# Adding two arrays and a GELU: a narrow load moved to the end of the loads

## The chip, the cores and the metric

The kernel runs on one core of a Trainium2 chip. The metric is the device time of one execution in microseconds (us), as a median of several runs. The profile is of one execution; its span is the time from the first to the last recorded event on the core.

## The reference

Two float32 arrays of 1024 x 4096 are added, and the tanh form of GELU is taken of the sum:

```python
def reference(x, y):
    z = x + y
    return (0.5 * z * (1 + np.tanh(np.sqrt(2 / np.pi) * (z + 0.044715 * z ** 3)))).astype(np.float32)
```

Every element is used once. 33.55 MB are read and 16.78 MB written.

## The kernel before

The arrays are taken as flat memory. On the chip the work is a plane of 128 partitions by TOT = 32,768 float32 columns, and `rows` (L90) says where a range of columns lies in memory: three blocks, columns 704 to 16,384 first, then 16,384 to 32,768, then columns 0 to 704 last. A row of a transfer is contiguous in memory.

There are two large tiles. `zt` (L128) has all 32,768 columns: x is loaded into it, the sum overwrites it, the GELU overwrites that, and the stores read it. `yt` (L129) has half the columns, 16,384: y's first half is loaded into it, and when its adds are done, y's second half is loaded over it. `ps` (L130) is a PSUM tile of 4,096 columns into which ScalarE copies some chunks of x, so that VectorE's add reads one operand from there and not both from the same memory as GpSimd's adds.

Transfers. x, y and the output are each moved in three pieces of 704, 15,680 and 16,384 columns. All nine are issued by SyncE (SP) on one queue, in the order of the list `sp` (L178): y's narrow piece, y's 15,680, x's narrow piece, x's 15,680, x's second half, y's second half; then the stores: the 15,680 columns, the narrow piece, the second half. SP works this list off in order, and an issue that waits holds up those behind it. y's second half waits for the adds of the chunks that still read `yt` (the `needs` entry of `load_y`, L186). A store waits for the GELUs of its columns (L193). After the build, `begin_early` (L9) puts the first two issues ahead of the start-up barrier, and `wait_late` (L23) lets only ScalarE wait for the last store.

Arithmetic. The columns are cut into 20 chunks (`chunks`, L103): two of 1,024, seven of 2,048, then from column 16,384 on 512, 1,536, six of 2,048, 1,024 and two of 512. Each chunk is added by VectorE (`on_vector`, L105) or GpSimd (`on_gpsimd`, L106: chunks 7, 8 and 12); chunk 7's add is held until chunk 1's is done (`held`, L108). Chunks 2 to 6 and 9 to 11 are first copied to PSUM by ScalarE (`copies`, L104). ScalarE also takes all GELUs. Its order, `on_scalar` (L107), is written out by hand: the five copies of the first half, the GELUs of chunks 0 and 1, the three copies of the second half, then the GELUs of chunks 2 to 19. Each engine takes its list in order; a loop (L200 to L210) only emits the instructions in an order that respects `needs`, and semaphores make the engines wait at run time.

Of the kernel before, what the change touches and what calls it, by code (L numbers as in the profile page):

```python
# [8 lines left out]
def begin_early(nc, count):  # L9


    head, body = (b.instructions for b in nc.main_func.blocks[:2])
    SP = mybir.EngineType.SP
    moved = [i for i in body if i.engine == SP and isinstance(i, mybir.InstDMACopy)][:count]
    assert not any(i.sync_info and i.sync_info.on_wait for i in moved)
    assert all(i.regs_accessed() == ((), ()) for i in moved)
    at = next(k for k, i in enumerate(head) if i.engine == SP)
    for k, i in enumerate(moved):
        body.remove(i)
        head.insert(at + k, i)  # L20
# [45 lines left out]
@with_exitstack  # L66
def kernel(
    ctx: ExitStack,
    tc: tile.TileContext,
    x: bass.AP,  # L70
    y: bass.AP,
    out: bass.AP,
):

    nc = tc.nc  # L80
    P = nc.NUM_PARTITIONS
    fp32 = mybir.dt.float32
    act = mybir.ActivationFunctionType

    N, D = x.shape
    assert N % P == 0
    TOT = N // P * D
    blocks = [(704, 16384), (16384, TOT), (0, 704)]

    def rows(array, lo, hi):  # L90
        flat, at = array.rearrange("n d -> (n d)"), 0
        for f, e in blocks:
            if f <= lo and hi <= e:
                own = flat[P * at : P * (at + e - f)].rearrange("(p c) -> p c", p=P)
                return own[:, lo - f : hi - f]
            at += e - f
        raise AssertionError((lo, hi))

    HALF = TOT // 2
    xloads = [704, 15680, HALF]  # L100
    yloads = [704, 15680, HALF]
    stores = [704, 15680, HALF]
    chunks = [1024, 1024] + [2048] * 7 + [512, 1536] + [2048] * 6 + [1024, 512, 512]  # L103
    copies = {2: 0, 3: 2048, 4: 0, 5: 2048, 6: 0, 9: 0, 10: 512, 11: 2048}  # L104
    on_vector = [0, 1, 2, 3, 4, 5, 6, 9, 10, 11, 13, 14, 15, 16, 17, 18, 19]  # L105
    on_gpsimd = [7, 8, 12]  # L106
    on_scalar = [("copy", c) for c in (2, 3, 4, 5, 6)] + [("gelu", 0), ("gelu", 1)] + [("copy", c) for c in (9, 10, 11)] + [("gelu", c) for c in range(2, 20)]  # L107
    held = {7: 1}  # L108

    def ranges(sizes):  # L110
        ends = [sum(sizes[: i + 1]) for i in range(len(sizes))]
        assert ends[-1] == TOT
        return [(e - f, e) for e, f in zip(ends, sizes)]

    xr, yr, sr, cr = (ranges(r) for r in (xloads, yloads, stores, chunks))
    C = len(cr)
    assert sorted(on_vector + on_gpsimd) == list(range(C))
    assert sorted(c for what, c in on_scalar if what == "gelu") == list(range(C))

    def over(rs, lo, hi):  # L120
        return [i for i, (a, b) in enumerate(rs) if a < hi and b > lo]

    pool_sb = ctx.enter_context(tc.tile_pool(name="xz", bufs=1))
    pool_y = ctx.enter_context(tc.tile_pool(name="y", bufs=1))
    pool_ps = ctx.enter_context(tc.tile_pool(name="ps", bufs=1, space=bass.MemoryType.PSUM))

    one = pool_sb.tile([P, 992], fp32, tag="one", name="one")
    zt = pool_sb.tile([P, TOT], fp32, tag="z", name="z")  # L128
    yt = pool_y.tile([P, HALF], fp32, tag="y", name="y")  # L129
    ps = pool_ps.tile([P, 4096], fp32, tag="ps", name="ps")  # L130
    adds = {}

    def in_psum(c):
        a, b = cr[c]
        return ps[:, copies[c] : copies[c] + b - a]

    def load_x(i):
        a, b = xr[i]
        nc.sync.dma_start(out=zt[:, a:b], in_=rows(x, a, b))  # L139

    def load_y(i):
        a, b = yr[i]
        o = a % HALF
        nc.sync.dma_start(out=yt[:, o : o + b - a], in_=rows(y, a, b))  # L144

    def store(i):
        a, b = sr[i]
        nc.sync.dma_start(out=rows(out, a, b), in_=zt[:, a:b])

    def copy(c):  # L150
        a, b = cr[c]
        nc.scalar.copy(out=in_psum(c), in_=zt[:, a:b])  # L152

    def add(c):
        a, b = cr[c]
        o = a % HALF
        eng = nc.gpsimd if c in on_gpsimd else nc.vector
        first = in_psum(c) if c in copies else zt[:, a:b]
        ins = eng.tensor_add(out=zt[:, a:b], in0=first, in1=yt[:, o : o + b - a])  # L159
        adds[c] = ins.ins  # L160
        if c in held:
            tc.add_manual_dep(
                ins.ins,
                adds[held[c]].name,
                mybir.DependencyInfo(mybir.DependencyClass.Sync, mybir.DependencyReason.DATA),
                reason="GpSimd's adds run beside VectorE adds that read one operand from PSUM",
            )

    def gelu(c):
        a, b = cr[c]  # L170
        nc.scalar.activation(out=zt[:, a:b], in_=zt[:, a:b], func=act.Gelu_apprx_tanh)  # L171

    def earlier_user(c):
        lo, hi = copies[c], copies[c] + chunks[c]
        before = [k for k in copies if k < c and copies[k] < hi and copies[k] + chunks[k] > lo]
        return [(add, k) for k in before]

    sp = [(load_y, 0), (load_y, 1), (load_x, 0), (load_x, 1), (load_x, 2), (load_y, 2)]  # L178
    sp += [(store, i) for i in (1, 0, 2)]
    pool = [(add, c) for c in on_gpsimd]  # L180
    dve = [(add, c) for c in on_vector]
    acts = [(gelu if what == "gelu" else copy, c) for what, c in on_scalar]

    needs = {
        load_x: lambda i: [],
        load_y: lambda i: [(add, c) for c in over(cr, yr[i][0] - HALF, yr[i][1] - HALF)],  # L186
        copy: lambda c: [(load_x, i) for i in over(xr, *cr[c])] + earlier_user(c),
        add: lambda c: [(load_x, i) for i in over(xr, *cr[c])]
        + [(load_y, i) for i in over(yr, *cr[c])]
        + [(copy, k) for k in copies if k == c]  # L190
        + [(add, k) for h, k in held.items() if h == c],
        gelu: lambda c: [(add, c)],
        store: lambda i: [(gelu, c) for c in over(cr, *sr[i])],  # L193
    }
    queues = [sp, pool, acts, dve]
    done = set()
    with tc.manual_schedule():
        nc.vector.memset(one[:, :1], 0.0)  # L198
        nc.scalar.activation(out=one[:, :1], in_=one[:, :1], func=act.Gelu_apprx_tanh)  # L199
        while any(queues):  # L200
            moved = False
            for q in queues:
                while q and all(n in done for n in needs[q[0][0]](q[0][1])):
                    fn, arg = q.pop(0)
                    fn(arg)
                    done.add((fn, arg))
                    moved = True
                    if q is not sp:
                        break
            assert moved, [q[:1] for q in queues]  # L210

    ctx.close()
    tc.close()
    tc.compile()  # L214
    begin_early(nc, 2)
    wait_late(nc)
# [30 lines left out]
```

## Time and profile before

| | us |
|---|---|
| median of 3 runs | 120.46 (120.14 to 120.53) |
| the profiled execution | 120.13 |
| its span | 118.6 |
| VectorE busy (DVE) | 29.1 |
| ScalarE busy (ACT) | 44.1 |
| GpSimd busy (POOL) | 13.8 |
| 2,048-column GELU, mean | 1.895 |
| 2,048-column add on VectorE, mean | 2.28 |
| 2,048-column add on GpSimd, mean | 4.54 |

Times of instructions are from the span's start. A group's line in the profile gives line, engine, operation, the tile written and the tiles read with their shapes, and how often. In a timeline the first two numbers are start and length in us, and the bracket is the idle time before it with what ended it. "SPq" is SyncE's queue, whose work is to issue transfers. For a transfer, "to landing" is the time from its issue until its semaphore says that all of it has arrived; on a queue with other transfers ahead of it, that includes their time. The packet records are the trace's list of the single packets, each with its start, length and size; a packet here is one row of a transfer.

### The profile page before, as it was taken

To read this page: it belongs to the slowest core of one execution; us is meant where nothing else is said; L and a number is where in the kernel's file an instruction comes from. 1 tells how busy PE (TensorE), PEld (TensorE's weight loads), DVE (VectorE), ACT (ScalarE), POOL (GpSimd) and SP (SyncE) were. 2 spreads that over 40 slices of the span, in tenths; PEclk is the share of its full clock that TensorE was granted. 3 is DMA by queue.
4 is the path that set the end of the run, shared out by engine and by line. 5 is a ranking of instruction groups with operands and counts; after the bars stand their busy time and mean duration, and the time that the engine had idled before them with its cause. 6 is when DMAs were issued, how large, how long until landed. Compare 5 with 4: busy or idle time off the path is not lost.

```text
span 118.6 us, 119 instructions
## 1 busy us (share of the span) xinstructions
DVE 29.1 (25%) x18; ACT 44.1 (37%) x30; POOL 13.8 (12%) x7
## 2 busy tenths in 40 slices
DVE  0000000000000099994000000009999920000000
ACT  5000000000000196792059999904799980000000
POOL 0000000000000029970000000009500000000000
DMA  9779977999789888988899889977997789988891
GB/s 460 338 338 571 444 338 338 460 571 444 338 360 656 354 354 376 663 376 354 354 597 464 354 354 508 552 338 338 529 486 338 338 385 517 619 354 354 354 663 44
DMA packets 1296, 50.33 MB, mean 424 GB/s; under 512 B 144, under 2 KB 144, under 8 KB 528
## 3 DMA queue, kind: packets, MB, share of 16 engines
q1 hardware_dynamic: 1296, 50.33, 98.6%
HBM read 33.55 MB, written 16.78 MB: 424 GB/s over the span
## 4 chain that ended last, share of the span: by engine, by line
DMA 55%; DVE 14%; ACT 10%; DVEq 1%; ACTq 0%; SPq 0%; issue 0%
DMA z<-in_x_dram 33%; DMA y<-in_y_dram 21%; DVE z L159 14%; ACT z L171 10%; DVEq L214 1%; ACTq L214 0%; SPq L139 0%; DVEq L159 0%; SPq L144 0%
## 5 line engine op out<-in xcount | busy, mean ns | idle before, releaser
L171 ACT ACTIVATE z<-z 128x2048 f32<-128x2048 f32 (+3 forms) x20 | 29.7, 1555 | 5.6 <-DVE z L159 5.6
L152 ACT COPY ps<-z 128x2048 f32<-128x2048 f32 (+2 forms) x8 | 13.0, 1654 | 46.6 <-DMA z<-in_x_dram 44.9
L159 DVE TENSOR_TENSOR z<-z,y 128x2048 f32<-128x2048 f32 (+2 forms) x9 | 13.6, 1574 | 39.9 <-DMA z<-in_x_dram 39.9
L159 DVE TENSOR_TENSOR z<-ps,y 128x2048 f32<-128x2048 f32 (+2 forms) x8 | 15.6, 2016 | 25.4 <-DMA y<-in_y_dram 25.4
L159 POOL TENSOR_TENSOR z<-z,y 128x2048 f32<-128x2048 f32 x3 | 13.6, 4538 | 70.6 <-DVE z L159 43.3
L199 ACT ACT_TABLE_LOAD x1 | 1.3, 1283 | 1.3 <-PEq L231 1.3
L198 DVE MEMSET one<- 128x1 f32 x1 | 0.1, 59 | 1.3 <-PEq L231 1.3
L199 ACT ACTIVATE one<-one 128x1 f32<-128x1 f32 x1 | 0.2, 202 | 0.0
L231 POOL MEMSET const-float32-0.0<- 128x1 f32 x1 | 0.1, 99 | 0.2 <-issue 0.2
L231 POOL MEMSET const-bfloat16-1.0<- 128x1 bf16 x1 | 0.1, 101 | 0.0
L231 POOL MEMSET const-uint8-127<- 128x1 uint8 x1 | 0.1, 101 | 0.0
L231 POOL MEMSET const-float32-1.0<- 128x1 f32 x1 | 0.1, 98 | 0.0
## 6 DMA issues: line engine op xcount, KB each, us to landing
y<-in_y_dram SPq DMA_DIRECT2D x1, 7840.0 KB, 21.2
z<-in_x_dram SPq DMA_DIRECT2D x1, 7840.0 KB, 39.5
out_dram<-z SPq DMA_DIRECT2D x1, 7840.0 KB, 21.4
y<-in_y_dram SPq DMA_DIRECT2D x1, 352.0 KB, 2.8
z<-in_x_dram SPq DMA_DIRECT2D x1, 352.0 KB, 21.3
out_dram<-z SPq DMA_DIRECT2D x1, 352.0 KB, 21.9
z<-in_x_dram SPq DMA_DIRECT2D x1, 58.3
y<-in_y_dram SPq DMA_DIRECT2D x1, 25.2
```

Of the source, the lines that this page charges most:

```text
L152: nc.scalar.copy(out=in_psum(c), in_=zt[:, a:b])
L159: ins = eng.tensor_add(out=zt[:, a:b], in0=first, in1=yt[:, o : o + b - a])
L171: nc.scalar.activation(out=zt[:, a:b], in_=zt[:, a:b], func=act.Gelu_apprx_tanh)
L198: nc.vector.memset(one[:, :1], 0.0)
L199: nc.scalar.activation(out=one[:, :1], in_=one[:, :1], func=act.Gelu_apprx_tanh)
L214: tc.compile()
L231: nc = _bacc.Bacc("TRN2", target_bir_lowering=False, num_devices=1)
```

## The change

x's narrow piece is no longer loaded third but sixth, behind y's second half, and so it is the last load. Chunk 0 now is those 704 columns (it had 1,024), and chunk 1 has 1,344. y's narrow piece is still the first load, but goes into a tile of its own, `ys`, where it waits; so y's second half no longer waits for chunk 0's add. VectorE adds chunk 0 after chunk 11 and ahead of chunk 13, and ScalarE takes its GELU after chunk 12's. The order of the stores is as before.

```diff
-    HALF = TOT // 2
-    xloads = [704, 15680, HALF]
-    yloads = [704, 15680, HALF]
-    stores = [704, 15680, HALF]
-    chunks = [1024, 1024] + [2048] * 7 + [512, 1536] + [2048] * 6 + [1024, 512, 512]
+    HALF, SLIM = TOT // 2, 704
+    xloads = [SLIM, 15680, HALF]
+    yloads = [SLIM, 15680, HALF]
+    stores = [SLIM, 15680, HALF]
+    chunks = [704, 1344] + [2048] * 7 + [512, 1536] + [2048] * 6 + [1024, 512, 512]
...
-    on_vector = [0, 1, 2, 3, 4, 5, 6, 9, 10, 11, 13, 14, 15, 16, 17, 18, 19]
+    on_vector = [1, 2, 3, 4, 5, 6, 9, 10, 11, 0, 13, 14, 15, 16, 17, 18, 19]
     on_gpsimd = [7, 8, 12]
-    on_scalar = [("copy", c) for c in (2, 3, 4, 5, 6)] + [("gelu", 0), ("gelu", 1)] + [("copy", c) for c in (9, 10, 11)] + [("gelu", c) for c in range(2, 20)]
+    on_scalar = [("copy", c) for c in (2, 3, 4, 5, 6)] + [("gelu", 1)] + [("copy", c) for c in (9, 10, 11)] + [("gelu", c) for c in [*range(2, 13), 0, *range(13, 20)]]
...
     yt = pool_y.tile([P, HALF], fp32, tag="y", name="y")
+    ys = pool_y.tile([P, SLIM], fp32, tag="ys", name="ys")
...
+    def in_y(a, b):
+        return ys[:, a:b] if b <= SLIM else yt[:, a % HALF : a % HALF + b - a]
+
     def load_y(i):
         a, b = yr[i]
-        o = a % HALF
-        nc.sync.dma_start(out=yt[:, o : o + b - a], in_=rows(y, a, b))
+        nc.sync.dma_start(out=in_y(a, b), in_=rows(y, a, b))
...
-        ins = eng.tensor_add(out=zt[:, a:b], in0=first, in1=yt[:, o : o + b - a])
+        ins = eng.tensor_add(out=zt[:, a:b], in0=first, in1=in_y(a, b))
...
-    sp = [(load_y, 0), (load_y, 1), (load_x, 0), (load_x, 1), (load_x, 2), (load_y, 2)]
+    sp = [(load_y, 0), (load_y, 1), (load_x, 1), (load_x, 2), (load_y, 2), (load_x, 0)]
     sp += [(store, i) for i in (1, 0, 2)]
...
-        load_y: lambda i: [(add, c) for c in over(cr, yr[i][0] - HALF, yr[i][1] - HALF)],
+        load_y: lambda i: [(add, c) for c in over(cr, yr[i][0] - HALF, yr[i][1] - HALF) if cr[c][1] > SLIM],
```

More of the change, by code (lines that the diff above doesn't have):

```diff
@@ L155, in add @@
         a, b = cr[c]
-        o = a % HALF
         eng = nc.gpsimd if c in on_gpsimd else nc.vector
         first = in_psum(c) if c in copies else zt[:, a:b]
-        ins = eng.tensor_add(out=zt[:, a:b], in0=first, in1=yt[:, o : o + b - a])
+        ins = eng.tensor_add(out=zt[:, a:b], in0=first, in1=in_y(a, b))
         adds[c] = ins.ins
```

## The prediction

> **What bounds the kernel now.** I read the page first: the queue table, the DMA row of the slices and the chain's shares say which resource is full.
>
> ```profile
> span 118.6 us, 119 instructions
> DMA  9779977999789888988899889977997789988891
> q1 hardware_dynamic: 1296, 50.33, 98.6%
> DMA 55%; DVE 14%; ACT 10%; DVEq 1%; ACTq 0%; SPq 0%; issue 0%
> ```
>
> One queue moves all 50.33 MB, and its packets fill 98.6% of sixteen engines' span. The 1.7 us that are left (1.4% of 118.6) lie at the ends: by the trace's packet records the first packet starts 0.99 us after the span's start, and the last ends 0.4 us before its end. The chain gives DVE 14% and ACT 10%, which looks as if arithmetic carried a quarter of the time. To test this I read when each transfer is issued (timeline of SyncE's queue; columns: start, duration) and how long it takes to land (the page's DMA issues, last column).
>
> ```profile
> 0.42 0.42 SPq L144 DMA_DIRECT2D y<-in_y_dram  x1
> 1.25 0.33 SPq L139 DMA_DIRECT2D z<-in_x_dram  x1
> 54.70 0.33 SPq L144 DMA_DIRECT2D y<-in_y_dram  x1
> 97.53 0.33 SPq L148 DMA_DIRECT2D out_dram<-z  x1
> ...
> y<-in_y_dram SPq DMA_DIRECT2D x1, 352.0 KB, 2.8
> z<-in_x_dram SPq DMA_DIRECT2D x1, 352.0 KB, 21.3
> out_dram<-z SPq DMA_DIRECT2D x1, 352.0 KB, 21.9
> z<-in_x_dram SPq DMA_DIRECT2D x1, 58.3
> y<-in_y_dram SPq DMA_DIRECT2D x1, 25.2
> ```
>
> The lines without a size are the 16,384-column transfers. Landings, worked out as issue plus duration: y's 15,680 columns 0.42 + 21.2 = 21.6; x's 704 columns 1.25 + 21.3 = 22.6; x's 15,680 columns 41.2 (the chain); x's second half 2.13 + 58.3 = 60.4; y's second half 54.70 + 25.2 = 79.9; first large store 76.97 + 21.4 = 98.4; narrow store 99.3; last store 97.53 + 21.1 = 118.6. From one landing to the next a 16,384-column transfer takes 19.3 to 19.5 us, and the last store lands 19.4 us after the narrow one. So nothing is lost between them: the queue runs through and the end is the bytes. The chain names arithmetic only because it follows the release of an issue, not the queue.
>
> What remains is how near arithmetic comes to starving the queue. The timeline of the second half:
>
> ```profile
> 64.24 12.70 ACT L171 ACTIVATE z<-z 128x2048 f32<-128x2048 f32 x7
> 76.97 20.89 SPq L148 DMA_DIRECT2D out_dram<-z  x3
> 80.03 4.53 POOL L159 TENSOR_TENSOR z<-z,y 128x2048 f32<-128x2048 f32 x1 [27.27 <-DMA y<-in_y_dram]
> 84.49 11.23 DVE L159 TENSOR_TENSOR z<-z,y 128x2048 f32<-128x2048 f32 x7
> 84.61 12.89 ACT L171 ACTIVATE z<-z 128x2048 f32<-128x2048 f32 x9 [0.71 <-DVE z L159]
> ```
>
> The ninth of the last GELUs ends at 97.50, the last store is issued at 97.53, and its first packets start at 98.37 (packet records), 0.84 us after the issue. Nine engines, done with the narrow store 0.1 us or less before, waited for it. The two slowest engines began it at 98.93 straight behind their own narrow packets. The slack of the store that ends the run is therefore 98.93 - 98.37 = 0.56 us. The other two hand-overs have more: y's second half is issued at 54.70 and needed when x's second half drains at 59.5 on the fastest engine (slack 59.5 - 54.70 - 0.84 = 4.0); the first large store is issued at 76.97 and needed at 78.9 (slack 1.1).
>
> **The change part by part.**
>
> Bytes and transfers. The nine transfers stay, with the same sizes. x's 704 columns go from behind y's first block to behind y's second half. In the middle of the full queue they cost an engine 8 packets of 0.112 us, 0.90 us (packet records; by landings, 704 x 19.4 / 16,384 = 0.83). Everything from x's 15,680 columns to y's second half starts 0.90 us earlier; the stores start where they did. On the queue: -0.90 + 0.90 = 0.
>
> Price at the new place. There the narrow reads stand between 64 KB reads and 62.7 KB writes, which the trace does not show. Lower end: the last large reads of y at the present turn took up to 2.74 us against 2.42 for the rest (packet records); on the two engines that end last they were 0.32 and 0.12 longer, and both hand over at 79.57. If the narrow reads take the turn and nothing is stretched, the later of the two gains 0.12. Upper end: the very first narrow load landed after 2.8 us for 0.83 of transfer, 2.0 more, on an empty queue. I take 0: the nearest rows are the narrow load amid reads (22.6 - 21.6 = 1.0) and the narrow store amid writes (99.3 - 98.4 = 0.9), both about their bytes.
>
> The Trainium skill's page "DMA: Bandwidth & Descriptors", section "Anatomy of one DMA — SWDGE (gpsimd) path", fits a transfer as some 2.0 us fixed plus bytes over 436 GB/s (on another issuing path than this queue's), and says the fixed part is mostly completion. By that the narrow load is 2.8 us, and the sum +2.0 if the fixed part were exposed at the turn. The trace agrees for the first load and not for the ones that stand in the queue, so the sum above goes without it.
>
> SyncE. Two issues are in new places. x's narrow load is issued straight behind y's second half, with no wait of its own, so only the first large store stands behind it and that waits until 76: an issue of 0.33 to 0.46 us costs nothing; uncovered it would cost just that. The narrow store, formerly issued at 77.4, now waits for its GELU, with only the last store behind it.
>
> First half. Data arrive at 41.16 - 0.90 = 40.26. VectorE now has one add of 1,344 columns, 1.22 (the 1,024-column form) + 320 x 1.04 ns = 1.55, in place of two of 1,024 (2.36), so it ends at 41.9 and not 43.65. The add of chunk 2 then needs its PSUM copy (40.28 + 1.87 = 42.2) and starts at 42.2 in place of 43.56; five of them take 11.07 as before and end at 53.3. GpSimd, released at 41.9, ends at 51.0. y's second half is issued at 53.4, x's second half drains at 58.6: slack 58.6 - 53.4 - 0.84 = 4.4. No effect.
>
> First large store. Copies start at 60.55 - 0.90 = 59.65, take 3.76, and seven GELUs 12.70: 76.1. The loads, narrow one included, still end at 78.9 on the fastest engine: slack 2.0 in place of 1.1. No effect.
>
> Second half. y lands at 79.0. Adds 9 to 11 end at 84.57 - 0.90 = 83.67, GpSimd's at 83.66. Then VectorE does the moved add, 0.683 (512 columns) + 192 x 1.05 ns = 0.88, or 0.80 from start to start; its x landed at 79.9, 3.7 us before. The rest starts at 84.4, not 84.49. ScalarE starts its last run at 84.61 - 0.90 = 83.71 and has one GELU more, of 704 columns: 0.618 (512 columns) + 192 x 0.83 ns = 0.78, some 0.68 from start to start. It ends at 97.50 - 0.90 + 0.68 = 97.28. VectorE does not get in its way: its fourth 2,048 add ends at 93.28, ScalarE asks for it at 93.41. So the last store is issued 0.22 us earlier, its slack is 0.78, the nine engines no longer wait, and the two slowest, which set the end, start as before.
>
> Sum: 0 on the queue, 0 at the turn, 0 from arithmetic. The profiled execution took 120.13 us (its 118.6 span and 1.5 around it); the median of the runs shown is 0.33 higher. On the median's scale that stays 120.46, and I say 120.4.
>
> **The rivals.**
>
> Turn dearer (slower). The narrow reads at the change from reading to writing do not stream at 0.112 us each but expose latency, as the first load did. For: the first load's 2.0 us, with packets up to 0.57 us long. Against: it met an empty queue, while here reads stand ahead and the first store is issued 2 us before. It decides from 0.36 us on; between that and the 2.0 it gives 120.8 to 122.5, likeliest 121.0.
>
> Turn cheaper (faster). The stretch of y's last large reads falls away, 0.12, and the engines come out of the turn more even. At the end of the run the last packets end between 117.71 and 118.25 us, in the mean at 117.85 (packet records); drawn fully even, the end comes 0.40 earlier, and the last store's new issue time allows that (97.28 + 0.84 + 19.4 = 117.5, where the present one stops at 97.53 + 0.84 + 19.4 = 117.8). So 0.12 to 0.40: 120.06 to 120.34. For: a third of the worst lag arose at this turn. Against: the same spread, 0.62 us, is there when x's second half drains (59.51 to 60.13), before anything that the change touches but its narrow load.
>
> Last store late (slower). The moved add and GELU sit ahead of the last chunks. If they, or a late landing of x's narrow rows, push the last GELU past 97.28 + 0.78 = 98.06, each further us is a us. A landing would have to be 3.7 us late to hold VectorE at all. With 1 us over: 121.4.
>
> That the load is not last in effect is excluded by the 4.4 us of slack at the issue of y's second half.
>
> **How the numbers follow.** No change: 0.66. Turn cheaper: 0.14, 0.04 of it under 0.3%, the rest near its upper end with the scatter of the runs on its side. Turn dearer: 0.14. Last store late: 0.06. Faster by over 0.3% (0.36 us, about what a measurement of this kernel can tell from none) is thus 0.10, within it 0.66 + 0.04 = 0.70, slower 0.14 + 0.06 = 0.20. The range, 119.95 to 121.2, takes in the whole cheaper turn and the dearer one to just past its likeliest; outside lie the upper part of the dearer turn and of the late store. For no change alone it is 120.1 to 120.7, the scatter of the runs shown with a little more above.
>
> **What would show it.** Right: x's first large block lands near 40.3, y's second half is issued near 53.4 and lands near 79.0, the first large store is issued near 76.1, the last near 97.3, with a span of 118.4 to 118.8 and the queue above 98%. The narrow load lands about 0.9 us behind y's second half. Wrong: the narrow load landing 1.5 us or more behind it, or the first large store landing later than 98.7, would be the turn; the last store issued after 98.1 would be arithmetic; a span below 118.3 would be the cheaper turn.

## The result, and the profile after

The changed kernel took 121.00 us (median of 22 executions, 120.68 to 121.84), the kernel before 120.19 (22 executions beside it). The ratio is 1.0061, 95% interval 1.0041 to 1.0081: slower by 0.7 us. The ratio and its interval, here and below, are of fast executions alone, those within 1.5% of the fastest of their kernel; the medians, which are of all, lie 0.8 us apart. The profiled execution of the changed kernel took 120.94 us, with a span of 119.5.

From the page of the changed kernel, with the lines of its DMA issues (last column: us from issue to landing; the last line, that of the last store, stands only in the fuller list of issues):

```profile
span 119.5 us, 118 instructions
q1 hardware_dynamic: 1296, 50.33, 98.6%
...
z<-in_x_dram SPq DMA_DIRECT2D x1, 7840.0 KB, 38.9
out_dram<-z SPq DMA_DIRECT2D x1, 7840.0 KB, 23.1
ys<-in_y_dram SPq DMA_DIRECT2D x1, 352.0 KB, 2.9
z<-in_x_dram SPq DMA_DIRECT2D x1, 352.0 KB, 27.1
out_dram<-z SPq DMA_DIRECT2D x1, 352.0 KB, 11.2
z<-in_x_dram SPq DMA_DIRECT2D x1, 58.0
y<-in_y_dram SPq DMA_DIRECT2D x1, 26.5
out_dram<-z SPq DMA_DIRECT2D x1, 21.4
```

SyncE's issues in the changed kernel, from its timeline (start, length):

```profile
1.26 0.33 SPq L140 DMA_DIRECT2D z<-in_x_dram  x1
1.64 0.52 SPq L140 DMA_DIRECT2D z<-in_x_dram  x1
53.23 0.33 SPq L147 DMA_DIRECT2D y<-in_y_dram  x1
53.61 0.43 SPq L140 DMA_DIRECT2D z<-in_x_dram  x1
76.13 0.35 SPq L151 DMA_DIRECT2D out_dram<-z  x1
88.87 0.34 SPq L151 DMA_DIRECT2D out_dram<-z  x1
98.05 0.33 SPq L151 DMA_DIRECT2D out_dram<-z  x1
```

The queue is still full for 98.6% of the span, with the same bytes and the same number of packets, and yet it is longer. Landings, issue plus duration, say where: x's second half at 1.64 + 58.0 = 59.6, y's second half at 53.23 + 26.5 = 79.7, x's narrow piece at 53.61 + 27.1 = 80.7, the first large store at 76.13 + 23.1 = 99.2, the last store at 98.05 + 21.4 = 119.4. Before, y's second half landed 19.5 us behind x's; now it is 20.1. The narrow load then takes 1.0, about its bytes. The first large store lands 0.8 us later than before, and the last store too.

The packet records narrow it down further. Of the eight 64 KB rows of y that each of the sixteen engines reads, seven take 2.42 us as before. The eighth, the last, takes 3.16 us in the mean and up to 3.47; before it was 2.47 and up to 2.74. Together with 0.12 in the narrow rows behind them an engine loses 0.86 us in the mean, against 0.06 before. That is the whole difference: the last packet of the run ends at 119.08 in place of 118.26. What the run's end follows is the slowest engine, not the mean. Call it a hand-over when an engine begins its first row of the first large store: the last engine hands over at 80.40 in place of 79.57, and from there to the end of the last 64 KB row are 38.68 us in both.

"Busy" in the queue table therefore hides it: a packet that takes 3.4 us in place of 2.4 counts as busy all the time.

### The profile page after: what moved, and what is told of

It is laid out like the page before. It is cut to its first block, busy times and chain, and to the rows that moved or that the text cites. A ratio compares the mean times of both kernels' runs of the same rounds, so it can differ in the third digit from the quotient of the medians.

```text
span 119.5 us, 118 instructions
## 1 busy us (share of the span) xinstructions
DVE 29.2 (24%) x18; ACT 44.1 (37%) x30; POOL 13.8 (12%) x7
## 3 DMA queue, kind: packets, MB, share of 16 engines
q1 hardware_dynamic: 1296, 50.33, 98.6%
## 4 chain that ended last, share of the span: by engine, by line
DMA 55%; ACT 13%; DVE 10%; DVEq 3%; issue 0%; ACTq 0%; SPq 0%
DMA z<-in_x_dram 33%; DMA y<-in_y_dram 22%; ACT z L173 11%; DVE z L161 10%; DVEq L216 3%; ACT ps L155 2%; ACTq L216 0%; DVEq L161 0%; SPq L147 0%
## 5 line engine op out<-in xcount | busy, mean ns | idle before, releaser
L173 ACT ACTIVATE z<-z 128x2048 f32<-128x2048 f32 (+5 forms) x20 | 29.7, 1555 | 6.2 <-DVE z L161 6.2
L161 DVE TENSOR_TENSOR z<-z,y 128x2048 f32<-128x2048 f32 (+3 forms) x8 | 12.8, 1664 | 38.9 <-DMA z<-in_x_dram 38.9
L161 DVE TENSOR_TENSOR z<-z,ys 128x704 f32<-128x704 f32 x1 | 0.9, 882 | 0.0
## 6 DMA issues: line engine op xcount, KB each, us to landing
z<-in_x_dram SPq DMA_DIRECT2D x1, 7840.0 KB, 38.9
out_dram<-z SPq DMA_DIRECT2D x1, 7840.0 KB, 23.1
z<-in_x_dram SPq DMA_DIRECT2D x1, 352.0 KB, 27.1
y<-in_y_dram SPq DMA_DIRECT2D x1, 26.5
```

The lines of the kernel that those rows point to most:

```text
L161: ins = eng.tensor_add(out=zt[:, a:b], in0=first, in1=in_y(a, b))
```

## The experiments

The first question was whether the narrow load at the turn from reading to writing is the cause. One kernel (e1) undoes only its place:

```diff
-    sp = [(load_y, 0), (load_y, 1), (load_x, 1), (load_x, 2), (load_y, 2), (load_x, 0)]
+    sp = [(load_y, 0), (load_y, 1), (load_x, 1), (load_x, 2), (load_x, 0), (load_y, 2)]
```

> The changed kernel with one thing undone: x's narrow load goes back ahead of y's second half; the tile ys, the chunks and the late add and GELU stay. Theory (the turn): the 0.8 us came from narrow reads standing between y's last large reads and the first store. Without them y's last 64 KB reads take 2.42 to 2.5 us each again, and the time is that of the kernel before, 120.2 to 120.4 (the last GELU ends near 98.2, some 0.1 us too late for the slowest queues). Rival (arithmetic, tile or chunks): the order of the loads is not the cause, and the time stays at 121.0.

Measured: 121.53 us, ratio 1.0104 (1.0070 to 1.0138). Not the time of the kernel before; its median lies even above that of the changed kernel, though the two intervals overlap. With no narrow read near it, y's last row took 2.97 us in the mean. So my first theory fell at once. (That its profiled execution ends 0.3 us later than the changed kernel's, with less stretch, 0.55 us, has a second cause: y lands 1.0 us later and the GELU of chunk 0 still stands behind chunk 12's, so the last store is issued at 99.04, its packets start at 99.88, and by then all sixteen engines wait for it.)

Two kernels add a load to the kernel before, x's 704 columns again into a tile `extra`, behind (e2) or ahead of (e3) y's second half:

```diff
-    sp = [..., (load_x, 2), (load_y, 2)]
+    sp = [..., (load_x, 2), (load_y, 2), (load_again, 0)]      # behind
+    sp = [..., (load_x, 2), (load_again, 0), (load_y, 2)]      # ahead
```

> The kernel before with one load more: x's 704 columns once again, into a tile that nobody reads, issued behind y's second half. Its bytes cost 0.9 us in any place. Theory (the turn): bytes plus the turn, 0.9 + 0.8, so 1.7 us over the kernel before, with y's last large reads stretched to 3.0 us and more. Rival (nothing special about the place): 0.9 us over, the same as with the extra load ahead of y's second half.

> The kernel before with the same extra load of 704 columns, issued ahead of y's second half and not behind it. Both theories: its bytes alone, 0.9 us over the kernel before, with y's last large reads as they were. The difference to the kernel with the extra load behind y's second half is the price of the place: 0.8 by the theory of the turn, 0 by its rival.

Measured: behind 122.18 us, 1.0182 (1.0130 to 1.0234); ahead 121.93, 1.0140 (1.0087 to 1.0193). The intervals overlap, so the price of the place is not shown, and both cost more than their bytes: 0.9 us is 0.75%, the rest 1.1% and 0.65%. That the load ahead of y costs more than its bytes is what neither theory had. In both profiled executions rows of y's last round are stretched: in e3 by 0.34 us an engine, in e2 by 0.11, but there one row took 3.05 us, and the last engine handed over at 81.23, so 1.66 later than before where the bytes are 0.9. What the two share with the changed kernel is that the loads end later as seen from the first store's issue. The fourth kernel (e4) moved that issue, by leaving out most of one GELU:

```diff
     def gelu(c):
         a, b = cr[c]
+        b = a + 8 if c == 8 else b
```

> The changed kernel with the GELU of chunk 8 cut to 8 columns (the rest of that chunk is stored without GELU), so that the first large store is issued some 1.8 us earlier, near 74.3, while y's last but one large reads are under way. Theory A (the order in the queue): the stretch stays on y's last reads and is as large, time 121.0. Theory B (the moment of the issue: handing a store to the queue disturbs the reads then in flight): the stretch moves to the reads ahead of the last ones, or falls away, with the time between 120.2 and 121.0.

Measured: 121.06 us, 1.0081 (1.0052 to 1.0110). The stretch stayed on the last rows, as theory A has it, but it was larger, as neither theory has it: 3.43 us in the mean for the last row and 0.27 in the narrow ones, 1.29 an engine in all. The median rose less than that; the profiled execution, 121.33, is one of the longer ones, and in it the last engine hands over at 80.78 and the last packet ends 1.21 us later than before.

So the theory became: a store that already waits in the queue while the last loads run stretches their last reads, and what counts is its lead, the time from its issue to the moment when the loads would end unstretched. Before, the lead was 2.1 us (issue 76.97, loads' end 79.06 in the mean over the engines). In the changed kernel it is 3.0: x's second half lands 0.84 us sooner, so the copies and GELUs that follow it and the store's issue come 0.84 sooner, while the loads, unstretched, would end when they did. The second set tests that against two rivals: that the engines' idleness does it, and that the narrow store no longer being issued right behind the large one does it. The issue is shifted with spare passes of ScalarE into an unused tile, as here in e5, or with a GELU cut short as in e4; the four kernels are e5 to e8, in this order:

```diff
     def gelu(c):
         a, b = cr[c]
+        for n in (992, 992) * (c == 8):
+            nc.scalar.activation(out=one[:, :n], in_=zt[:, 704 : 704 + n], func=act.Gelu_apprx_tanh)
         nc.scalar.activation(out=zt[:, a:b], in_=zt[:, a:b], func=act.Gelu_apprx_tanh)
```

> The changed kernel with two spare ScalarE passes of 992 columns (about 0.92 us each, into the unused tile) ahead of the GELU of chunk 8, so that the first large store is issued 1.8 us later, near 78.0, still early enough for its first packets (78.0 + 0.84 = 78.8 against 79.0 to 79.2 when the loads end). T1 (lead: a store that waits in the queue while the last loads run stretches their last reads, the more the longer it waits): the stretch falls from 0.9 us an engine to under 0.2 and the time to 120.2 to 120.4. T2 (idle engines: the stretch comes while ScalarE has nothing to do): also less, since ScalarE is busy 1.8 us longer. T3 (the narrow store is no longer issued right behind the large one): no difference, 121.0.

> The kernel before with the GELU of chunk 8 cut to 8 columns (the rest of that chunk is stored without GELU), so that its first large store is issued 1.7 us earlier, near 75.2. Order and width of all transfers are those of the kernel before. T1: y's last reads are stretched by 0.5 to 1.3 us, time 120.8 to 121.5. T2: the same, ScalarE being idle from 75.2. T3: no difference, 120.2, as the narrow store follows at once.

> The changed kernel with three spare ScalarE passes of 992 columns (2.8 us) behind the GELU of chunk 8: the first large store is issued at 76.1 as before, but ScalarE is busy until 78.9, past most of the stretch. T1 and T3: no difference, 121.0, with y's last reads stretched to 3 us and more. T2: 120.2 to 120.5.

> The kernel before with one spare ScalarE pass of 800 columns (0.76 us) ahead of the GELU of chunk 8: its first large store is issued near 77.7, needed at 78.9 less 0.84, so 0.3 us of slack. T1: the little stretch that is left (0.06 us an engine in its profile) goes, 120.1 to 120.2, and the executions of the kernel before that lie above 121 become rare. T2 and T3: no difference.

The changed kernel with the store issued later (e5), its issues and their time to landing:

```profile
53.26 0.33 SPq L147 DMA_DIRECT2D y<-in_y_dram  x1
78.05 0.35 SPq L151 DMA_DIRECT2D out_dram<-z  x1
...
out_dram<-z SPq DMA_DIRECT2D x1, 7840.0 KB, 20.2
y<-in_y_dram SPq DMA_DIRECT2D x1, 25.7
```

120.03 us, 1.0008 (0.9992 to 1.0024). More work, and the whole loss is gone: y lands at 53.26 + 25.7 = 79.0, the moment that the prediction gave, and the last rows take 2.42 us. And the kernel before with the store issued earlier (e6):

```profile
54.93 0.33 SPq L144 DMA_DIRECT2D y<-in_y_dram  x1
75.50 0.83 SPq L148 DMA_DIRECT2D out_dram<-z  x2
...
out_dram<-z SPq DMA_DIRECT2D x1, 7840.0 KB, 24.4
y<-in_y_dram SPq DMA_DIRECT2D x1, 26.4
```

121.60 us, 1.0123 (1.0092 to 1.0154). Less work, the old order of loads, the narrow store right behind the large one, and it is slower by 1.5 us. y lands at 81.3; its last rows take 3.52 us.

The kernel with ScalarE kept busy after an early issue (e7) stayed slow, 120.77 us, 1.0058 (1.0043 to 1.0072), above the 120.2 to 120.5 of T2. Its last rows took 2.65 us, with 0.34 more in the narrow ones; T1 had said 3 us and more. So the stretch is smaller than expected, but idleness is not the cause. The kernel before with the store issued 0.6 us later (e8) took 120.03, 0.9988 (0.9970 to 1.0007): no gain that can be told from none. Whether executions above 121 become rarer could not be seen, since none of the 19 of the kernel before beside it lay there either.

The third set asks for the law: does any store do it, does it grow without end, does the place of the narrow load matter at equal lead, and is the price in proportion? Its kernels are e9 to e12.

```diff
-    sp += [(store, i) for i in (1, 0, 2)]
+    sp += [(store, i) for i in (0, 1, 2)]      # e9, with a spare pass of 800 columns
...
+        b = a + 8 if c in (6, 7, 8) else b      # e10
```

The last two combine edits already shown: e11 is e1 with the two spare passes, e12 the changed kernel with one.

> The kernel before with the narrow store as the first store, so that it waits in the queue from about 55 on, 24 us before the loads end, and with the spare ScalarE pass of 800 columns ahead of the GELU of chunk 8 (large store issued near 77.6, some 2.3 us before it is needed). Any store that waits stretches the loads: y's last reads 1 us longer and more, time above 121. Only the lead of a large store counts: stretch under 0.1 us an engine, 120.0 to 120.2.

> The kernel before with the GELUs of chunks 6, 7 and 8 cut to 8 columns each (the rest of them is stored without GELU): first large store issued near 71.8, some 7.3 us before the loads end. If only an engine's last read is stretched, the price is full at 1.1 to 1.3 us, and the time 121.2 to 121.6, as with the store issued at 75.5. If every read under way while a store waits is stretched by the same share (about 0.4), it grows to 2.5 us and more: 122.5 or above.

> The changed kernel with x's narrow load back ahead of y's second half, and with two spare ScalarE passes of 992 columns ahead of the GELU of chunk 8, so that the first large store is issued near 78.1. If the lead is the cause, the place of the narrow load plays no part: 120.0 to 120.4, where without the spare passes it took 121.5. If the order of the loads costs something of its own, it stays above 121.

> The changed kernel with one spare ScalarE pass of 992 columns ahead of the GELU of chunk 8: first large store issued near 77.1, so 2.1 us before the loads end, the lead that the kernel before has. By the lead: 120.1 to 120.3, the time of the kernel before, with a stretch of 0.05 to 0.2 us an engine. If the cost came in proportion to the lead: 120.6.

The narrow store early (e9), its issues:

```profile
54.55 0.33 SPq L144 DMA_DIRECT2D y<-in_y_dram  x1
54.99 0.38 SPq L148 DMA_DIRECT2D out_dram<-z  x1
77.62 0.34 SPq L148 DMA_DIRECT2D out_dram<-z  x1
...
y<-in_y_dram SPq DMA_DIRECT2D x1, 25.8
```

121.58 us, 1.0089 (1.0047 to 1.0132); y lands at 80.4, and its last rows took 3.17 us in the mean. A store of 352 KB that waits is enough; the large one behind it had a lead of 1.5 us, at which e8 showed no stretch. ScalarE's work is that of e8, so its idleness is not the cause here either. The kernel with the store issued at 71.84 (e10):

```profile
54.67 0.33 SPq L144 DMA_DIRECT2D y<-in_y_dram  x1
71.84 0.82 SPq L148 DMA_DIRECT2D out_dram<-z  x2
...
out_dram<-z SPq DMA_DIRECT2D x1, 7840.0 KB, 27.7
y<-in_y_dram SPq DMA_DIRECT2D x1, 26.3
```

121.50 us, 1.0091 (1.0056 to 1.0126). The lead is 7.2 us and the stretch 1.27: the price is full. The rows read before the last one take 2.42 to 2.44 us although the store waits beside them too. Only an engine's last large read, and what narrow reads follow it, are stretched.

The kernel with the narrow load back ahead of y's second half and the store late (e11) took 120.60, 0.9996 (0.9957 to 1.0036). That is above the 120.0 to 120.4 expected, but the kernel before took 120.37 beside it. No row is stretched, so at a short lead the place of the narrow load costs nothing that shows; the interval would hide 0.4%. The changed kernel with one spare pass (e12):

```profile
53.29 0.33 SPq L147 DMA_DIRECT2D y<-in_y_dram  x1
53.66 0.44 SPq L140 DMA_DIRECT2D z<-in_x_dram  x1
77.03 0.35 SPq L151 DMA_DIRECT2D out_dram<-z  x1
...
z<-in_x_dram SPq DMA_DIRECT2D x1, 352.0 KB, 26.1
y<-in_y_dram SPq DMA_DIRECT2D x1, 25.6
```

120.24 us, 0.9970 (0.9936 to 1.0004). So 0.9 us of lead makes the whole difference in time that shows between the two kernels of this study. The cost is not in proportion to the lead: the 120.6 of a proportion would be 0.2% above the kernel before beside it, outside the interval. Here x's narrow load lands 53.66 + 26.1 = 79.8, 0.9 us behind y's 53.29 + 25.6 = 78.9: at the turn it costs about its bytes.

All kernels, by lead. The lead is from the issue of the first store to the mean over the engines of when the loads would end, each engine's last 64 KB row taken at 2.42 us and a narrow load behind it at 0.90; the stretch is what an engine's last reads took beyond that, in the profiled execution. Each ratio is to the kernel before as it ran beside that kernel.

| kernel | first store issued | lead, us | stretch, us an engine | ratio to before |
|---|---|---|---|---|
| e11 (e1, store later) | 78.41 | 1.1 | 0.00 | 0.9996 |
| e5 (changed, store later) | 78.05 | 1.2 | 0.00 | 1.0008 |
| e8 (before, store later) | 77.59 | 1.5 | 0.01 | 0.9988 |
| e12 (changed, store a bit later) | 77.03 | 2.1 | 0.00 | 0.9970 |
| before | 76.97 | 2.1 | 0.06 | 1 |
| e2 (before, extra load behind y; 0.75% more bytes) | 77.17 | 2.9 | 0.11 | 1.0182 |
| e1 (changed, narrow load ahead of y; last store late too) | 76.25 | 3.0 | 0.55 | 1.0104 |
| changed kernel | 76.13 | 3.0 | 0.86 | 1.0061 |
| e7 (changed, ScalarE busy) | 76.03 | 3.1 | 0.57 | 1.0058 |
| e3 (before, extra load ahead of y; 0.75% more bytes) | 76.87 | 3.2 | 0.34 | 1.0140 |
| e6 (before, store earlier) | 75.50 | 3.7 | 1.10 | 1.0123 |
| e4 (changed, store earlier) | 74.43 | 4.7 | 1.29 | 1.0081 |
| e10 (before, store much earlier) | 71.84 | 7.2 | 1.27 | 1.0091 |
| e9 (before, narrow store early) | 54.99 | 24.1 | 0.75 | 1.0089 |

Up to 2.1 us the stretch is 0.06 or less, above 3.5 it is over 1 us for a large store. Around 3 it scatters, 0.11 to 0.86. The mean is also not what sets the time: in ten of the fourteen kernels the last packet ends 38.68 or 38.69 us after the last hand-over, so one slow engine is enough, as in e2. (The others are e9, where no narrow store follows the large one, with 37.81, e3 with 38.86, and e1 and e11, whose last store is issued late, with 38.92 and 38.98.) For e2, e3 and e9 the profiled execution was the shortest of its kernel, so their medians hold more than their stretches show.

Read engine by engine, the packet records place the edge. Where the store was issued 0.3 us or more before any engine began its last 64 KB row (e1, e3, e4, e6, e9, e10), 94 of the 96 rows took over 0.1 us longer. Where it was issued 0.7 us or more after all had begun it (e5, e8, e11, e12), none of the 64 took over 0.04 longer. In the kernel before, the changed kernel, e2 and e7 the issue fell in between; 3, 16, 3 and 9 of the 16 rows were over 0.1 us longer, and no run shows why these differ.

What stays open is why. One sentence of the Trainium skill, page "DMA: Bandwidth & Descriptors", section "Two DMAs through the same engine are not ordered", has an engine's read side and write side as separate queues whose descriptors are pipelined. By that an engine could already fetch a waiting store's rows while it still writes its last load. The trace agrees in that only the last reads are touched. It leaves open why a waiting load does no such thing (x's last rows took 2.42 us with y's second half issued 5 us before they ended), and no record here shows the store's own reads at that time, so it is an idea and not a finding.

## Why the prediction was wrong

It said no change, 120.4 in 119.95 to 121.2, and 0.70 for less than 0.3% of change. Measured were 0.6% and 121.0: inside the range, on the side to which 0.20 had been given. That it lies inside is luck: that part of the range stood for narrow reads that cost more at the turn, and they did not.

Right, by the changed kernel's rows: x's first block landed at 1.26 + 38.9 = 40.2 (40.3 said), y's second half was issued at 53.23 (53.4), the first large store at 76.13 (76.1), the narrow load came 1.0 us behind y (0.9), and the last store, at 98.05 and not 97.28, was late by 0.77 us, about the 0.74 by which y was. Instruction costs and the bytes on the queue held.

Wrong was the step "First large store", which ends "slack 2.0 in place of 1.1. No effect.", and with it the "0 at the turn" of the sum. I took a transfer's earlier issue into a full queue as free, since all that I asked of an issue was that it not come too late. The runs show that here it can come too early: with 0.84 us of extra lead y's last rows took 3.16 us in place of 2.47, the last hand-over came 0.82 us later and the time rose by 0.7 to 0.8; taking the lead back with one spare pass took all of that away (e12).

The rival "turn dearer" had the place right and its likeliest time, 121.0, was the time measured, but by luck. Of its two signs, the first large store landing later than 98.7 appeared (99.2), and the narrow load landing 1.5 us or more behind y did not (1.0). Its mechanism was wrong: the narrow reads did not expose a latency. e1 stretched without them, e5 and e12 had them and did not. The 2.0 us fixed part that the Trainium skill, page "DMA: Bandwidth & Descriptors", section "Anatomy of one DMA — SWDGE (gpsimd) path", fits to a transfer was not exposed either; e12's narrow load landed 0.9 us behind y at the same place.

The trace of the kernel before did hold a hint. I saw y's last rows longer than the others, up to 2.74 us against 2.42, and put it down to the turn as such, with its removal as the only way in which it could change. That it depended on when the store had been issued, and so could grow, I did not ask.

"Turn cheaper" gave 120.06 to 120.34 for a turn without stretch. With the lead short (e5, e8, e12) the turn was without it, and the gain was within what could be measured: 1.0008, 0.9988, 0.9970. None beats the kernel before for certain.

## What to carry to other kernels

Where one queue carries loads and then stores and is the bound, look at the last reads ahead of the first store packet by packet: if they are longer than the others, try issuing the first store later, up to when it is really needed. In this kernel a store issued up to 2.1 us ahead of the loads' end cost nothing that shows, and a large one issued 3.7 us or more ahead cost 1.0 to 1.5 us. A change that makes data arrive sooner can lose by it, since it moves issues as well; so list for every moved issue not only what it may be late for but what it now stands beside.

## What the runs showed of the hardware

I had not expected that a store which only waits in the queue lengthens loads ahead of it: an engine's last 64 KB read went from 2.47 us in the kernel before to 3.68 in the mean (e10), that a store of 352 KB is enough (e9, 3.17 us), or that the effect is confined to the last large read of each engine and what follows it, whatever the lead (the rows before it took 2.42 us in the mean in every kernel). The "busy" share of the queue does not tell: it was 98.6% in the kernel before, in the changed kernel and in e10.
